# An early store of sixteen zeroed rows ahead of a pooling kernel's main loop

## The chip, the cores and the metric

The kernel runs on one core of a Trainium2 chip. The metric is the device time of one execution in microseconds; the figure used is the median of several runs. Profiles are taken of one execution, and their times count from the first instruction of that execution.

Names used below: ACT is the scalar engine, DVE the vector engine, POOL is GpSimd, SP the engine that here only issues transfers. SBUF is the on-chip memory with 128 partitions, PSUM the smaller one beside it, DRAM the chip's main memory. A transfer (DMA) is issued from an engine's queue (here SP's, which the profile calls q1, or ACT's, q10) and carried out by 16 DMA engines.

## The reference

The reference is a one-dimensional pooling with the 2-norm over windows of four neighbours. With `x` of shape 32 x 256 x 4096 in float32 (134.2 MB), `p = 2` and `kernel_size = 4`:

```python
for i in range(out_length):
    start = i * kernel_size
    end = start + kernel_size
    window = np.abs(x[:, :, start:end]) ** p
    result[:, :, i] = (np.mean(window, axis=-1)) ** (1.0 / p)
```

So every output element is the square root of the mean of four squares. The output is 32 x 256 x 1024 in float32, 33.6 MB.

## The kernel before

Input and output are treated as flat. The input is cut into 20 tiles of 128 partitions. Most are W = 13184 columns wide (52,736 bytes to a partition, 6592 KB in all); tile 3 is 32 columns narrower, and tile 19 takes what is left (11680 columns). R = W / 4 = 3296 is the number of output columns of a full tile.

Tiles are grouped in blocks (`blocks`, L51): four blocks of four tiles, one of three (18, 16, 17) and the last tile alone. A block is one contiguous region of the flat input and of the flat output. Within it each partition owns one contiguous run, so one store writes the results of a whole block, 128 rows of up to 52,736 bytes. `rows(flat, b, div)` (L64) gives the view of block `b` in the input (`div` 1) or the output (`div` 4).

In SBUF there are three input tiles `xt` (L58), used in turn: tile `i` uses slot `i % 3`. The result tile `ot` (L59) has room for four tiles' results; tile `i` of the first 16 writes columns `i % 4 * R` onward (L70), so tiles 0, 4, 8 and 12 share columns 0 to 3295. The sums of tiles 4, 8, 12 and 16 go to a PSUM tile `st` instead, since the columns in `ot` are still being stored then, and their roots are written to `ot` later. Results of the last four tiles are held in a freed input slot.

Each tile passes through four steps:

- a load issued by SP (`load`, L79 to L83);
- the square in place on ACT (`square`, L89);
- two additions on DVE: `pairs` (L95) halves the row, `fours` (L99) writes the sum of four to the result's place;
- the square root with the factor 1/4 on ACT (`root`, L102), for one or several tiles at once.

The first three loads are issued ahead of the loop. After the sums of tile `i`, SP issues load `i + 3` into the slot that was just freed. The stores of blocks 0, 1 and 2 (`store`, L85 and L86) are issued from ACT's queue after the last root of the block, those of blocks 3, 4 and 5 from SP's.

The order is written out by hand: each engine executes its instructions in the order of the program text. Waits are inserted where one instruction touches what another engine or a transfer has written or reads. `implied` (L118) takes out a few of them that other waits cover. Transfers signal their end on eight semaphores that are used in turn. Ahead of the loop ACT computes the root of a constant into `first` (L129), and the load of its function table stands in front of that.

Of the kernel before, what the change touches and what calls it, by code (L numbers as in the profile page):

```python
# [1 line left out]

# [4 lines left out]


@with_exitstack
def kernel(  # L10
    ctx: ExitStack,
    tc: tile.TileContext,
    x: bass.AP,
    p: float,
    kernel_size: int,
    out: bass.AP,
):

    nc = tc.nc

    assert float(p) == 2.0, "kernel specialized for p == 2"
    k = int(kernel_size)  # L30
    assert k == 4, "kernel specialized for kernel_size == 4"

    P = nc.NUM_PARTITIONS
    fp32 = mybir.dt.float32
    Act = mybir.ActivationFunctionType
    add = mybir.AluOpType.add
    xf = x.rearrange("b c l -> (b c l)")
    of = out.rearrange("b c l -> (b c l)")
    total = xf.shape[0] // P

    W = 13184
    R = W // k
    X_SLOTS = 3
    NARROW = W - 32
    LAST = total - 18 * W - NARROW
    widths = [W] * 3 + [NARROW] + [W] * 15 + [LAST]
    n = len(widths)
    assert 0 < LAST <= W and LAST % 16 == 0


    blocks = [[0, 1, 2, 3], [4, 5, 6, 7], [8, 9, 10, 11], [12, 13, 14, 15], [18, 16, 17], [19]]  # L51
    block_of = {i: b for b, group in enumerate(blocks) for i in group}
    block_width = [sum(widths[i] for i in group) for group in blocks]

    x_pool = ctx.enter_context(tc.tile_pool(name="x_pool", bufs=1))
    o_pool = ctx.enter_context(tc.tile_pool(name="o_pool", bufs=1))
    s_pool = ctx.enter_context(tc.tile_pool(name="s_pool", bufs=1, space=bass.MemoryType.PSUM))
    x_tiles = [x_pool.tile([P, W], fp32, name=f"xt{j}") for j in range(X_SLOTS)]  # L58
    o_tile = o_pool.tile([P, 4 * R], fp32, name="ot")  # L59
    first = o_pool.tile([P, 1], fp32, name="first")  # L60
    s_tile = s_pool.tile([P, 4096], fp32, name="st")
    ctx.enter_context(tc.manual_schedule())

    def rows(flat, b, div):  # L64
        at = sum(block_width[:b]) * P // div
        return flat[at:at + block_width[b] * P // div].rearrange("(p w) -> p w", p=P)


    free = x_tiles[17 % X_SLOTS]
    place = {i: o_tile[:, i % 4 * R:i % 4 * R + widths[i] // k] for i in range(16)}  # L70
    place[18] = free[:, R:2 * R]
    place[19] = free[:, 0:LAST // k]
    place[16] = free[:, 2 * R:3 * R]
    place[17] = free[:, 3 * R:4 * R]
    held = [o_tile[:, 0:w // k] for w in block_width[:4]] + [free[:, R:4 * R], place[19]]

    xs, loads, stores, sums, squares = {}, {}, {}, {}, {}

    def load(i):  # L79
        b = block_of[i]  # L80
        at = sum(widths[j] for j in blocks[b][:blocks[b].index(i)])
        xs[i] = x_tiles[i % X_SLOTS][:, 0:widths[i]]
        loads[i] = nc.sync.dma_start(out=xs[i], in_=rows(xf, b, 1)[:, at:at + widths[i]])  # L83

    def store(b, queue):  # L85
        stores[b] = queue.dma_start(out=rows(of, b, k), in_=held[b])  # L86

    def square(v):
        return nc.scalar.activation(out=v, in_=v, func=Act.Square)  # L89

    def pairs(v):

        q = v.rearrange("p (n j) -> p n j", j=k)
        h = v[:, 0:v.shape[1] // 2].rearrange("p (n j) -> p n j", j=2)
        return nc.vector.tensor_tensor(out=h, in0=q[:, :, 0:2], in1=q[:, :, 2:4], op=add)  # L95

    def fours(o, v):
        h = v[:, 0:v.shape[1] // 2].rearrange("p (n j) -> p n j", j=2)
        return nc.vector.tensor_tensor(out=o, in0=h[:, :, 0], in1=h[:, :, 1], op=add)  # L99

    def root(o, s):
        return nc.scalar.activation(out=o, in_=s, func=Act.Sqrt, scale=1.0 / k)  # L102

    summed = {i: s_tile[:, 0:R] if i in (4, 8, 12, 16) else place[i] for i in range(n)}

    def roots(*group):
        if len(group) == 1:
            root(place[group[0]], summed[group[0]])
        else:
            v = o_tile[:, group[0] % 4 * R:(group[-1] % 4 + 1) * R]  # L110
            r = root(v, v)
            if group[0] in (5, 9):

                implied(r, stores[block_of[group[0]] - 1])
        if group[-1] in (3, 7, 11):
            store(block_of[group[-1]], nc.scalar)

    def implied(later, earlier):  # L118

        tc.declare_no_dep(later.ins, earlier.ins, reason="implied by the other waits")  # L120

    for i in range(X_SLOTS):
        load(i)


    ahead = {4: (3,), 8: (7,), 12: (11,)}
    behind = {3: [(0, 1, 2)], 7: [(5, 6), (4,)], 11: [(9, 10), (8,)], 14: [(12,)], 15: [(13, 14)], 16: [(15,)]}

    root(first[:, :], nc.const_aps.tensor(1.0, (P, 1), fp32))  # L129
    for i in range(17):  # L130
        if i in ahead:
            roots(*ahead[i])
        s = square(xs[i])
        squares[i] = s
        if i == 3:
            implied(s, squares[0])
        if i in (3, 7, 11):

            for earlier in sums[i - X_SLOTS]:
                implied(s, earlier)  # L140
        for group in behind.get(i, []):
            roots(*group)
        sums[i] = pairs(xs[i]), fours(summed[i], xs[i])
        if i + X_SLOTS < n:
            load(i + X_SLOTS)

    store(3, nc.sync)
    square(xs[17])
    pairs(xs[17])
    fours(summed[17], xs[17])  # L150
    later = {18: 4608, 19: 2000}

    def shared_square(i):
        v = xs[i][:, 0:later[i]]
        nc.vector.tensor_tensor(out=v, in0=v, in1=v, op=mybir.AluOpType.mult)  # L155
        square(xs[i][:, later[i]:widths[i]])

    def shared_pairs(i):
        implied(pairs(xs[i]), loads[i])

    shared_square(18)
    roots(16)
    roots(17)
    shared_pairs(18)
    fours(summed[18], xs[18])
    shared_square(19)
    roots(18)
    store(4, nc.sync)
    shared_pairs(19)
    fours(summed[19], xs[19])  # L170
    roots(19)
    store(5, nc.sync)


# [1 line left out]
_INS = ['x', 'p', 'kernel_size']  # L176
_OUTS = [((32, 256, 1024), 'float32')]

_NUMBERS = {'p': 2.0, 'kernel_size': 4}


# [26 lines left out]
```

## Time and profile before

| what | value |
|---|---|
| median of three runs | 393.97 us (393.89 to 394.08) |
| the profiled execution's span | 392.3 us |
| ACT busy | 274.4 us |
| DVE busy | 218.2 us |
| POOL busy | 0.2 us (four constants) |
| bytes read from and written to DRAM | 134.22 MB and 33.55 MB |
| issue to landing of the three stores from ACT's queue | 36.3 us for the first, median 35.1 us for the other two |

The span is the time between the first and the last instruction that the profiler recorded; it is 1.7 us below the median of the runs. A span on ACT or DVE is the time in which the engine executed. For transfers the profile shows their issue, their landing and, for each queue, the packets that the 16 DMA engines moved. One row of one transfer is one packet; packets under 512 bytes are the signals at a transfer's end, up to 16 for each. In the lists, `[16.56 <-DMA xt<-in_x_dram]` behind an instruction says how long its engine had been idle before it and what ended that.

### The profile page before, as it was taken

What the parts mean: (1) busy time and instruction counts of PE and PEld (TensorE: products, weight loads), DVE (VectorE), ACT (ScalarE), POOL (GpSimd) and SP (SyncE); (2) the same over time, 40 slices, a digit from 0 to 9 for tenths busy, and PEclk for the clock granted to TensorE, in tenths of its full rate; (3) what the DMA queues carried; (4) which work ended last, traced back from release to release, by engine and by line L of the source; (5) the groups of instructions that cost most, each with busy time, mean ns of one, the idle gap of its engine ahead of it and who ended that gap; (6) DMA issues with size and microseconds to landing.
All of it is one profiled execution on the core that took longest, in us unless ns stands there. A gap on an engine that the chain in (4) does not pass through costs nothing.

```text
span 392.3 us, 176 instructions
## 1 busy us (share of the span) xinstructions
DVE 218.2 (56%) x42; ACT 274.4 (70%) x37; POOL 0.2 (0%) x4
## 2 busy tenths in 40 slices
DVE  0009477580693274905942748069418485699970
ACT  1095695979950859799509597995098999969910
POOL 0000000000000000000000000000000000000000
DMA  8999999999999999999999999999999999999997
GB/s 344 430 430 430 430 440 435 452 457 366 430 430 430 430 430 430 430 441 446 452 446 441 436 430 436 430 430 430 430 430 430 430 430 430 430 453 415 430 413 342
DMA packets 3744, 167.77 MB, mean 428 GB/s; under 512 B 416, under 2 KB 416, under 8 KB 416
## 3 DMA queue, kind: packets, MB, share of 16 engines
q1 hardware_dynamic: 3312, 147.53, 87.4%
q10 hardware_dynamic: 432, 20.25, 11.9%
HBM read 134.22 MB, written 33.55 MB: 428 GB/s over the span
## 4 chain that ended last, share of the span: by engine, by line
DMA 43%; ACT 30%; DVE 23%; issue 0%; ACTq 0%; SPq 0%; DVEq 0%
DMA xt<-in_x_dram 43%; ACT xt L89 28%; DVE xt L95 14%; DVE ot L99 5%; DVE xt L99 3%; DVE xt L155 2%; ACT ot L102 2%; ACT xt L102 1%; ACTq L86 0%; SPq L83 0%; DVEq L95 0%
## 5 line engine op out<-in xcount | busy, mean ns | idle before, releaser
L89 ACT ACTIVATE xt<-xt 128x13184 f32<-128x13184 f32 (+3 forms) x20 | 216.7, 10847 | 92.3 <-DMA xt<-in_x_dram 91.0
L95 DVE TENSOR_TENSOR xt<-xt 128x6592 f32<-128x6592 f32 (+2 forms) x20 | 139.7, 6985 | 144.1 <-ACT xt L89 143.9
L99 DVE TENSOR_TENSOR ot<-xt 128x3296 f32<-128x3296 f32 (+1 forms) x13 | 46.7, 3592 | 17.9 <-DMA out_dram<-ot 17.6
L102 ACT ACTIVATE ot<-ot 128x6592 f32<-128x6592 f32 (+3 forms) x8 | 37.2, 4655 | 7.0 <-DVE ot L99 7.0
L102 ACT ACTIVATE xt<-xt 128x3296 f32<-128x3296 f32 (+1 forms) x3 | 8.5, 2836 | 8.8 <-DVE xt L99 8.8
L99 DVE TENSOR_TENSOR st<-xt 128x3296 f32<-128x3296 f32 x4 | 14.4, 3600 | 0.1
L99 DVE TENSOR_TENSOR xt<-xt 128x3296 f32<-128x3296 f32 (+1 forms) x3 | 10.4, 3461 | 0.1
L102 ACT ACTIVATE ot<-st 128x3296 f32<-128x3296 f32 x3 | 8.7, 2898 | 0.0
L155 DVE TENSOR_TENSOR xt<-xt 128x4608 f32<-128x4608 f32 (+1 forms) x2 | 7.2, 3593 | 0.0
L102 ACT ACTIVATE xt<-st 128x3296 f32<-128x3296 f32 x1 | 2.9, 2898 | 0.0
L102 ACT ACT_TABLE_LOAD x1 | 1.3, 1283 | 0.7 <-PEq L189 0.7
L102 ACT ACTIVATE first<-const-float32-1.0 128x1 f32<-128x1 f32 x1 | 0.2, 202 | 0.0
L189 POOL MEMSET const-bfloat16-1.0<- 128x1 bf16 x1 | 0.1, 101 | 0.0
L189 POOL MEMSET const-uint8-127<- 128x1 uint8 x1 | 0.1, 101 | 0.0
L189 POOL MEMSET const-float32-0.0<- 128x1 f32 x1 | 0.1, 98 | 0.2 <-issue 0.2
L189 POOL MEMSET const-float32-1.0<- 128x1 f32 x1 | 0.1, 98 | 0.0
## 6 DMA issues: line engine op xcount, KB each, us to landing
xt<-in_x_dram SPq DMA_DIRECT2D x18, 6592.0 KB, 29.8
out_dram<-ot ACTq DMA_DIRECT2D x2, 6592.0 KB, 35.1
out_dram<-ot SPq DMA_DIRECT2D x1, 6592.0 KB, 37.1
out_dram<-ot ACTq DMA_DIRECT2D x1, 6588.0 KB, 36.3
xt<-in_x_dram SPq DMA_DIRECT2D x1, 6576.0 KB, 24.7
xt<-in_x_dram SPq DMA_DIRECT2D x1, 5840.0 KB, 21.9
out_dram<-xt SPq DMA_DIRECT2D x1, 4944.0 KB, 16.1
out_dram<-xt SPq DMA_DIRECT2D x1, 1460.0 KB, 8.2
```

The costliest lines, as they stand in the source:

```text
L89: return nc.scalar.activation(out=v, in_=v, func=Act.Square)
L95: return nc.vector.tensor_tensor(out=h, in0=q[:, :, 0:2], in1=q[:, :, 2:4], op=add)
L99: return nc.vector.tensor_tensor(out=o, in0=h[:, :, 0], in1=h[:, :, 1], op=add)
L102: return nc.scalar.activation(out=o, in_=s, func=Act.Sqrt, scale=1.0 / k)
L155: nc.vector.tensor_tensor(out=v, in0=v, in1=v, op=mybir.AluOpType.mult)
L189: nc = _bacc.Bacc("TRN2", target_bir_lowering=False, num_devices=1)
```

## The change

Between the first three loads and the loop two instructions are added. GpSimd writes zeros to columns 0 to 3295 of the result tile in all 128 partitions. Then ACT issues a transfer from every eighth partition of these columns (partitions 0, 8, ..., 120) to the corresponding rows of block 0 of the output: 16 rows of 13,184 bytes, 210,944 bytes in all. The store of block 0 later writes the same place in the output with the results. In program order the new transfer precedes `first` on ACT.

```diff
     for i in range(X_SLOTS):
         load(i)
+    BULK = 3296
+    nc.gpsimd.memset(o_tile[:, 0:BULK], 0.0)
+    nc.scalar.dma_start(out=rows(of, 0, k)[0:P:8, 0:BULK], in_=o_tile[0:P:8, 0:BULK])
 
 
     ahead = {4: (3,), 8: (7,), 12: (11,)}
```

The new instructions bring these waits: the transfer waits for the memset; DVE's sum of tile 0 into the same columns waits for the memset and for the transfer; the root over tiles 0 to 2 waits for the transfer. The transfers after load 0 each use the next of the eight semaphores, compared with before. Everything else is unchanged.

## The prediction

> **What bounds the kernel now.** I read the page first, its slices and its queues.
>
> ```profile
> span 392.3 us, 176 instructions
> ...
> DVE 218.2 (56%) x42; ACT 274.4 (70%) x37; POOL 0.2 (0%) x4
> ...
> DMA  8999999999999999999999999999999999999997
> GB/s 344 430 430 430 430 440 435 452 457 366 430 430 430 430 430 430 430 441 446 452 446 441 436 430 436 430 430 430 430 430 430 430 430 430 430 453 415 430 413 342
> ...
> q1 hardware_dynamic: 3312, 147.53, 87.4%
> q10 hardware_dynamic: 432, 20.25, 11.9%
> ```
>
> No compute engine is above 70%, and the DMA digit is 9 in all slices but the first and the last. The two queues' packets take 87.4 + 11.9 = 99.3% of the time of 16 engines. So the DMA engines bound the kernel from end to end, although the chain of waits names ACT and DVE for half of its length. The timeline confirms it by when the squares (L89) start, which is when loads land:
>
> ```profile
> 0.73 1.28 ACT L102 ACT_TABLE_LOAD   x1 [0.73 <-PEq L189]
> 0.73 338.28 SPq L83 DMA_DIRECT2D xt<-in_x_dram  x20
> 2.02 0.20 ACT L102 ACTIVATE first<-const-float32-1.0 128x1 f32<-128x1 f32 x1
> 18.79 11.19 ACT L89 ACTIVATE xt<-xt 128x13184 f32<-128x13184 f32 x1 [16.56 <-DMA xt<-in_x_dram]
> ...
> 34.35 11.19 ACT L89 ACTIVATE xt<-xt 128x13184 f32<-128x13184 f32 x1 [4.38 <-DMA xt<-in_x_dram]
> 37.07 3.59 DVE L99 TENSOR_TENSOR ot<-xt 128x3296 f32<-128x3296 f32 x1
> ...
> 90.31 0.38 ACTq L86 DMA_DIRECT2D out_dram<-ot  x1
> ...
> 144.41 11.19 ACT L89 ACTIVATE xt<-xt 128x13184 f32<-128x13184 f32 x1 [4.36 <-DMA xt<-in_x_dram]
> ...
> 222.22 11.19 ACT L89 ACTIVATE xt<-xt 128x13184 f32<-128x13184 f32 x1 [4.38 <-DMA xt<-in_x_dram]
> ...
> 371.76 11.74 SPq L86 DMA_DIRECT2D out_dram<-xt  x2
> ```
>
> Loads 0 and 1 land 15.56 us apart. From load 7 (144.41) to load 11 (222.22) four loads and one full store go through in 77.81 us, 15.56 each: a store's byte costs what a load's does, and nothing is idle between. One full transfer is 128 rows of 52,736 bytes, 8 per engine if they are shared evenly, so 15.56 / 8 = **1.945 us per row and engine**. The end is saturated too: the last two stores are issued at 371.76 and about 383.2, and by the page's medians to landing (16.1 and 8.2 us) they land at 387.9 and 391.4. The 3.5 us between is the 1460 KB of the last at the full rate (15.56 x 1460 / 6592 = 3.45). Whatever keeps the slowest DMA engine busy longer therefore comes out at the end, undiminished.
>
> One stretch is not regular. From load 3 (65.47) to load 7 is 78.94 us for the same five transfers, 1.13 more than the next cycle. The third view, DMA in 12 us around the first store (issued at 90.31) and then around the second (169.29), shows where:
>
> ```profile
> DMA packets 103, 5.01 MB, mean 417 GB/s; under 512 B 8, under 2 KB 8, under 8 KB 8
> ...
> q1 hardware_dynamic: 71, 3.32, 72.2%
> q10 hardware_dynamic: 32, 1.69, 32.4%
> ...
> DMA packets 115, 5.27 MB, mean 439 GB/s; under 512 B 15, under 2 KB 15, under 8 KB 15
> ...
> q1 hardware_dynamic: 76, 3.22, 61.9%
> q10 hardware_dynamic: 39, 2.06, 39.5%
> ```
>
> In the first window 95 rows take 104.6% of 12 us x 16 engines, which is 2.11 us a row; in the second 100 rows take 101.4%, which is 1.95. The excess is 95 x 0.16 / 16 = about **1.0 us per engine**. It comes once, where ACT's queue (q10) is used for the first time; the second store has none.
>
> **The change, part by part.**
>
> *The memset.* GpSimd is free after its four constants at 0.43 us. No row shows 3296 columns on it. The bounds are its own 0.10 us for one column and, doubling the nearest row (DVE's 3.59 us for 3296 columns), 7.2 us. I take 3.6, so it ends near 4.3. Nothing else is on GpSimd, and DVE first works at 30.01.
>
> *ACT's queue.* The DMA waits for the memset and stands ahead of the table load (1.28) and `first` (0.20). With 0.38 us for the issue, ACT is through at 4.3 + 0.38 + 1.48 = 6.2 us, or 9.8 with the long memset. Its next work is the square at 18.79, so the waiting costs nothing. Were that cover gone, square 0 would be late and load 3 (issued at 40.70 once DVE has summed tile 0) with it; but load 2 feeds the engines until 49.94, another 9.2 us of cover.
>
> *New waits.* DVE's sum into columns 0 to 3295 (37.07) now waits for the memset and for the early store, and so does the root over tiles 0 to 2. Behind the sum stand load 3 on SP and all later sums. The first full store landed 36.3 us after its issue with 8 rows per engine, each taking turns with a load's. A quarter-length row issued near 4.7 should be in by 15, 22 us before it is needed. The later transfers move on by one among the eight DMA semaphores; load 6 waits for one that load 0 had finished. I cost these at nothing.
>
> *The bytes.* 16 rows of 13,184 bytes are 210,944 bytes that go to DRAM twice. A quarter row takes 1.945 / 4 = 0.486 us on one engine. The trace doesn't show which engine, or which path into the result tile, serves partitions 0, 8, 16 and so on. The ends are 0.49 us (one row to each, nothing shared) and, with two rows in each shared lane, 0.97 us. I take **0.97**, for a reason in the trace: the engines run nearly in step (in the windows their packet starts come in bursts every 1.95 us), so these rows move at the same time, and a load lands only when its last engine is through. If any pair shares a lane, the worst pair counts and not the mean.
>
> The Trainium skill has a rule for each end. "DMA: Bandwidth & Descriptors", section "Why a DMA increments its semaphore by 16 and not by 1", lets a transfer use the largest number of engines up to 16 that divides both sides' outermost size; for 16 rows that is 16 engines, and by it alone the term is 0.49. "SBUF — State Buffer", section "Door 1: The DMA port swizzle", makes bandwidth follow the ports that the partitions reach; partitions eight apart reach 8 of 16, and by it the term is 0.97. No row of this trace shows a transfer of fewer than 128 partitions, so neither is borne out here yet.
>
> *First use of q10.* The 1.0 us moves from 92 us to about 5 us. Engines are as saturated there (422 GB/s in each 2 us from 4 on), so it is paid there and given back at the first full store. Ends: -1.0 (it hides in the first load's own start) and +1.0 (paid at both). I take 0.
>
> **Sum.** Span 392.3 + 0.97 = 393.2. The median of the runs is 393.97, 1.7 above this span; the same distance gives **394.94**, which is 0.25% slower. The bound for telling it from no change is 0.2%, 0.79 us, so 394.76.
>
> **Rivals.**
>
> (a) One row to each engine and no shared lane: 393.97 + 0.49 = **394.46**, not slower by the bound. For it: every transfer here keeps 16 engines equally busy. Against: all of those have 128 rows. A partial overlap of pairs lies between, near 394.7.
>
> (b) The first-use cost comes twice, since q10 then stands idle from about 15 to 90 us: 394.46 + 1.0 to 394.94 + 1.0, **395.4 to 395.9**. Against: about 43 us of idleness (from the first store's landing at 126.6 to 169.3) brought no second one; 75 us is not shown.
>
> (c) The first-use cost hides in the start: the first load needs 18.06 us instead of 15.56, so 2.5 us there aren't transfer. **393.5 to 393.9**. Against: by 4 us the rate is full, and the memset most likely ends later; only a memset well under 3 us would bring the store in earlier.
>
> (d) Few engines take all the rows: four of them with 4 rows each give 1.94 us, 395.9; one with 16 gives 16 x 0.486 = 7.8, **401.8**. Nothing in the trace speaks for it.
>
> (e) The early store waits behind the three queued loads and lands at 50. DVE's sum would be 13 us late, load 3 issued near 53.6 instead of 40.7, and the engines idle for some 4 to 5 us: **about 399**. Against: the first full store landed at 126.6, before load 6, which had been issued ahead of it and landed at 128.86.
>
> **How the numbers follow.** Forecast 0.40; (a) with the partial overlaps 0.31; (b) 0.14; (c) 0.09; (d) and (e) together 0.04; something that I don't see and that is faster, 0.02. The forecast lies only 0.18 us above the bound, so I count 0.03 of it as no change. Slower: 0.37 + 0.14 + 0.04 = 0.55. No change: 0.31 + 0.03 + 0.08 = 0.42. Faster: 0.03, since even (c) at its best is -0.5 us, 0.12%. The range takes in (a), the forecast and (b): 394.2 to 395.9; it leaves out (c), (d), (e) and a little of (b).
>
> **What would show it.** In the changed kernel's profile: load 0 landing near 19.7 instead of 18.79 (19.3 by (a)), plus up to 1.0 if first use is paid there; the cycle from load 3 to load 7 back at 77.8 instead of 78.94; the later cycles unchanged; DVE's first sum not waiting for a DMA; and the memset over well before 10 us. The early store's landing less than 11 us after its issue would clear (e). I am wrong if the cycle from load 3 to load 7 keeps its 1.1 us, or if load 0 is late by no more than the first use and half a microsecond.

## The result and the profile after

The changed kernel takes 394.97 us (median of 9 runs, 394.66 to 395.57) against 393.97 us before (393.87 to 394.18). The ratio is 1.0026, interval 1.0018 to 1.0034: slower by 1.0 us. The profiled execution has a span of 393.0 us; it took 395.06 us.

The page of the changed kernel, slices and queues:

```profile
span 393.0 us, 181 instructions
...
DMA  9999999999999999999999999999999999999997
...
q1 hardware_dynamic: 3312, 147.53, 87.2%
q10 hardware_dynamic: 464, 20.46, 12.0%
```

The engines that move data are as full as before: 99.2% over a span that is 0.7 us longer. q10 has 32 packets more, 16 rows and 16 signals, so 16 engines took part in the early store. The timeline of the changed kernel:

```profile
0.73 2.84 POOL L125 MEMSET ot<- 128x3296 f32 x1 [0.29 <-POOLq L192]
...
3.61 0.58 ACTq L126 DMA_DIRECT2D out_dram<-ot  x1
4.22 1.28 ACT L102 ACT_TABLE_LOAD   x1 [4.22 <-POOL ot L125]
...
19.41 11.19 ACT L89 ACTIVATE xt<-xt 128x13184 f32<-128x13184 f32 x1 [13.69 <-DMA xt<-in_x_dram]
...
37.76 3.59 DVE L99 TENSOR_TENSOR ot<-xt 128x3296 f32<-128x3296 f32 x1
...
66.11 11.16 ACT L89 ACTIVATE xt<-xt 128x13152 f32<-128x13152 f32 x1 [4.34 <-DMA xt<-in_x_dram]
...
144.97 11.19 ACT L89 ACTIVATE xt<-xt 128x13184 f32<-128x13184 f32 x1 [4.41 <-DMA xt<-in_x_dram]
...
222.82 11.19 ACT L89 ACTIVATE xt<-xt 128x13184 f32<-128x13184 f32 x1 [4.40 <-DMA xt<-in_x_dram]
```

The memset and the issue are over long before ACT has anything else to do, and DVE's first sum stands without an idle time in front of it, so the new waits cost no time in the loop. Load 0 lands at 19.41 instead of 18.79, 0.62 later; load 3 is late by 0.64, load 7 by 0.56, load 11 by 0.60. The loss inside the span is made in the first 19 us and carried to the end. The cycle from load 3 to load 7 takes 78.86 us, hardly less than the 78.94 before.

The DMA view of the first 12 us of the changed kernel, queue by queue (packets, MB, share of 16 engines):

```profile
q1 hardware_dynamic: 80, 4.22, 88.1%
q10 hardware_dynamic: 32, 0.21, 4.2%
...
out_dram<-ot ACTq DMA_DIRECT2D x1, 206.0 KB, 8.0
```

The same view of the kernel before:

```profile
q1 hardware_dynamic: 80, 4.22, 87.2%
```

4.2% of 12 us is 0.50 us per engine, signal included: each row takes what a quarter of a 1.945 us row takes, 0.49 us, and no more. In the trace's list of packets each of them follows another load row without a gap, one on each of the 16 engines. The load rows' 88.1% against 87.2% says little. The kernel with the memset and no transfer (below) shows as much in its first 12 us:

```profile
q1 hardware_dynamic: 80, 4.22, 88.0%
```

The first row of an engine takes some 2 to 3 us, and how long varies from run to run. A small price does show in the list of packets: the load row just ahead of an early row took up to 2.30 us instead of 1.95. This is 0.14 us per engine on average here and 0.07 in a second profile of the same kernel; with the memset alone these rows take 1.95 us on every engine. So load 0's delay of 0.62 us is the 0.49 of the early row and about 0.1 of stretched load rows and scatter. The scatter is not small: in the six kernels that move no extra bytes, load 0 landed between 18.79 and 18.95 us five times, and once at 19.30. Nothing here took twice its time.

Inside the span this leaves 0.6 to 0.7 us of the 1.0. The rest is outside: over all runs of this study the time lay about 1.8 us above the span for the kernel before (1.74 to 1.84), and 2.02 to 2.09 us above it in the nine runs of the changed one. One run of all that follow, of the kernel with 16 neighbours, was in a slower state (401.21 us) and is left out of the table.

### The profile page after: what moved, and what is told of

Its sections match the earlier page's. It is cut to its first block, busy times and chain, and to the rows that moved or that the text cites. A ratio compares the mean times of both kernels' runs of the same rounds, so it can differ in the third digit from the quotient of the medians.

```text
span 393.0 us, 181 instructions
## 1 busy us (share of the span) xinstructions
DVE 218.2 (56%) x42; ACT 274.4 (70%) x37; POOL 3.0 (1%) x5
## 3 DMA queue, kind: packets, MB, share of 16 engines
q1 hardware_dynamic: 3312, 147.53, 87.2%
## 4 chain that ended last, share of the span: by engine, by line
DMA 43%; ACT 30%; DVE 23%; issue 0%; ACTq 0%; DVEq 0%; SPq 0%
DMA xt<-in_x_dram 43%; ACT xt L89 28%; DVE xt L95 14%; DVE ot L99 5%; DVE xt L99 3%; DVE xt L158 2%; ACT ot L102 2%; ACT xt L102 1%; ACTq L86 0%; SPq L83 0%; DVEq L95 0%; DVEq L99 0%
## 5 line engine op out<-in xcount | busy, mean ns | idle before, releaser
L89 ACT ACTIVATE xt<-xt 128x13184 f32<-128x13184 f32 (+3 forms) x20 | 216.7, 10847 | 89.3 <-DMA xt<-in_x_dram 88.1
L125 POOL MEMSET ot<- 128x3296 f32 x1 | 2.8, 2844 | 0.3 <-POOLq L192 0.3
```

The source lines that it names most:

```text
L125: nc.gpsimd.memset(o_tile[:, 0:BULK], 0.0)
```

## The experiments

Each was timed in five rounds beside the kernel before on the same chip. "Distance" is the median of time less span over the runs; the last column is the number of instructions that the trace records on DVE, with those that only wait.

| kernel | time | before | ratio, interval | span (before) | distance (before) | DVE |
|---|---|---|---|---|---|---|
| changed kernel again | 395.06 | 394.05 | 1.0024, 1.0015 to 1.0034 | 393.0 (392.3) | 2.05 (1.77) | 54 |
| memset alone | 394.35 | 394.05 | 1.0007, 0.9998 to 1.0016 | 392.3 (392.3) | 2.05 (1.77) | 54 |
| short rows | 394.46 | 394.05 | 1.0010, 1.0001 to 1.0019 | 392.4 (392.3) | 2.07 (1.77) | 54 |
| 16 neighbours | 394.91 | 394.05 | 1.0024, 1.0013 to 1.0034 | 392.8 (392.3) | 2.07 (1.77) | 54 |
| one column on GpSimd | 394.22 | 393.93 | 1.0007, 0.9998 to 1.0016 | 392.2 (392.1) | 2.05 (1.81) | 54 |
| memset on DVE | 394.96 | 393.93 | 1.0024, 1.0015 to 1.0032 | 392.8 (392.1) | 2.17 (1.81) | 55 |
| two rows | 394.58 | 393.93 | 1.0013, 1.0005 to 1.0022 | 392.5 (392.1) | 2.04 (1.81) | 54 |
| narrow tile at 7 | 394.03 | 393.93 | 1.0003, 0.9994 to 1.0012 | 392.2 (392.1) | 1.81 (1.81) | 53 |
| `first` twice | 394.11 | 394.04 | 1.0000, 0.9991 to 1.0009 | 392.3 (392.25) | 1.79 (1.79) | 53 |
| many rows | 394.91 | 394.04 | 1.0022, 1.0013 to 1.0031 | 392.9 (392.25) | 2.03 (1.79) | 54 |
| constant rows | 394.15 | 394.04 | 1.0001, 0.9992 to 1.0010 | 392.4 (392.25) | 1.77 (1.79) | 53 |
| store on SP, spare column | 394.73 | 394.04 | 1.0020, 1.0011 to 1.0029 | 392.7 (392.3) | 2.07 (1.80) | 54 |

### Taking the change apart: no transfer, the whole, short rows

The changed kernel was run again as it is:

> The changed kernel once more, beside runs of the kernel before whose spans are listed. Expected +1.0 us in time again. If the whole loss is DMA work inside the span, the spans differ by as much as the times; the trace so far shows only 0.6 to 0.7 us inside (load 0 lands 0.62 later), so the rest, 0.3 to 0.4, may lie outside or be the scatter of single executions.

It lost 1.0 us again, 0.7 in the span and 0.28 outside it. Next, without the transfer:

```diff
-    nc.scalar.dma_start(out=rows(of, 0, k)[0:P:8, 0:BULK], in_=o_tile[0:P:8, 0:BULK])
```

> The memset stays, the early transfer is gone. If all of the loss comes from the transfer, the time is that of the kernel before, within 0.2 us, and load 0 lands at 18.8. If GpSimd's memset itself or the wait on ACT costs something outside the profiled span, the time is 0.3 to 0.5 us above the kernel before with the span unchanged.

The span is that of before, and the time is 0.30 us higher. The interval of the ratio just takes in 1, but the distances don't overlap: 2.02 to 2.10 us in the eleven runs, 1.74 to 1.83 in the 28 of the kernel before. The memset takes 2.85 us in which nothing waits for it; the price is outside the profiled span. Then the transfer with short rows:

```diff
-    nc.scalar.dma_start(out=rows(of, 0, k)[0:P:8, 0:BULK], in_=o_tile[0:P:8, 0:BULK])
+    nc.scalar.dma_start(out=rows(of, 0, k)[0:P:8, 0:128], in_=o_tile[0:P:8, 0:128])
```

> The same 16 partitions with 512 bytes in each instead of 13,184, so the bytes' own time is 0.02 us per engine. If the loss is the bytes, 0.49 us of it goes and what stays is the change-over between queues, 0.1 to 0.2 us. If a transfer has a fixed price on the engines or outside the span, most of the 1.0 us stays.

This adds 0.11 us to the memset alone, which is about the scatter: the medians of the kernel before differ by 0.12 us between the rounds. Going from 512 to 13,184 bytes in a row adds the rest, 395.06 - 394.46 = 0.60 us, close to the 0.49 us of a row and the 0.07 to 0.14 of stretched load rows read above. So the loss is 0.30 (outside the span) + 0.11 + 0.60 = 1.01 us, each part good to about 0.1.

### Do rows share a lane?

```diff
-    nc.scalar.dma_start(out=rows(of, 0, k)[0:P:8, 0:BULK], in_=o_tile[0:P:8, 0:BULK])
+    nc.scalar.dma_start(out=rows(of, 0, k)[0:16, 0:BULK], in_=o_tile[0:16, 0:BULK])
```

> The same 16 rows of 13,184 bytes, but partitions 0 to 15 in place of every eighth. Theory of shared lanes: sixteen neighbours reach fewer of the lanes than partitions eight apart, four rows to a lane, so the term grows to about 4 x 0.49 = 1.9 us and load 0 lands near 20.8. Theory of one row to an engine with nothing shared: each row again takes 0.49 us, load 0 lands at 19.4, the time is that of the changed kernel.

The time is that of the changed kernel within 0.15 us, and the 1.9 us of the theory are not there. Some sharing shows all the same. In the first 12 us of this kernel:

```profile
q1 hardware_dynamic: 80, 4.22, 87.6%
q10 hardware_dynamic: 32, 0.21, 5.0%
```

q10's rows take 5.0% instead of 4.2%, 0.60 us each on average with the signal. In the trace eight of them take the plain 0.49 us and the others 0.56 to 0.79. For partitions eight apart every row took 0.49. So the rows of neighbours took a little longer and those of partitions eight apart did not. That neighbours share a path is one reading of it, from one profile; a doubling is shown for neither.

### Does the slowest engine set the end?

```diff
-    nc.scalar.dma_start(out=rows(of, 0, k)[0:P:8, 0:BULK], in_=o_tile[0:P:8, 0:BULK])
+    nc.scalar.dma_start(out=rows(of, 0, k)[0:16:8, 0:BULK], in_=o_tile[0:16:8, 0:BULK])
```

> Only partitions 0 and 8 are stored early: 2 rows of 13,184 bytes, an eighth of the bytes. If the slowest DMA engine sets the end, as the prediction has it, two engines that are each 0.49 us late cost as much as sixteen: span near 392.9, time near 394.9. If the bytes count as a sum over 16 engines, the term is 0.06 us and the time is that of the short rows, 394.46.

With an eighth of the bytes, on two engines (two rows and two signals, the four packets of q10 in the first 12 us below), the span still grows by 0.4 us of the 0.6 to 0.7.

```profile
q10 hardware_dynamic: 4, 0.03, 0.5%
```

The time, 394.58, lies between the two that were on record, 394.9 for the slowest engine and 394.46 for the sum, so it doesn't decide between them. The growth of the span is several times the 0.06 of a sum over 16 engines, and less than 0.49. The trace tells more. Load 0 is hardly late:

```profile
19.02 11.19 ACT L89 ACTIVATE xt<-xt 128x13184 f32<-128x13184 f32 x1 [12.72 <-DMA xt<-in_x_dram]
```

With the memset alone it landed at 18.91. In the list of packets the engines are up to 0.6 us apart at this point. The two that took the early rows began them at 8.40 and 8.46 us, when the slowest of the others had until 8.81 with its third load row. They were through at 8.89 and 8.95 and from then on the last, but by 0.14 us only. So the slowest engine does set the landing, as the prediction said, but an early row costs its whole 0.49 us only where it falls on the slowest engine, as it must when all 16 have one. In these two profiles the lateness is 0.11 us at load 0, 0.24 at load 11 and 0.3 at the end of the span; what adds to it on the way isn't shown.

### What costs time outside the span?

First one column on GpSimd and no transfer:

```diff
-    BULK = 3296
+    BULK = 1
     nc.gpsimd.memset(o_tile[:, 0:BULK], 0.0)
-    nc.scalar.dma_start(out=rows(of, 0, k)[0:P:8, 0:BULK], in_=o_tile[0:P:8, 0:BULK])
```

> No transfer, and GpSimd's memset writes one column in place of 3296. The memset alone left the span at 392.3 us but moved the time from 1.77 to 2.05 us above the span. Theory 1: what lies outside the span grows by one more GpSimd instruction that DVE waits for, whatever its size; the distance is 2.05 again, time 394.35. Theory 2: it grows with the memset's length (2.85 us of GpSimd work); the distance is back at 1.77, time 394.05.

The distance is 2.05 us, so the length of the memset has no part in it. Then the whole change with its memset on DVE:

```diff
-    nc.gpsimd.memset(o_tile[:, 0:BULK], 0.0)
+    nc.vector.memset(o_tile[:, 0:BULK], 0.0)
```

> The changed kernel with the memset on DVE in place of GpSimd; the transfer is unchanged. If the 0.28 us outside the span belong to GpSimd, the distance from span to time is back at 1.77 us, the span stays near 393.0 and the time is 394.75. If any added instruction costs this, distance 2.05 and time 395.05. DVE is free until 30 us, so the span is not expected to change for the memset's sake.

Both guesses failed: the distance is larger, 2.17. It isn't GpSimd's. Then one more instruction on ACT in the kernel before:

```diff
     root(first[:, :], nc.const_aps.tensor(1.0, (P, 1), fp32))
+    root(first[:, :], nc.const_aps.tensor(1.0, (P, 1), fp32))
```

> The kernel before with the root of a constant into the tile first executed twice: one more small instruction, on ACT, and nothing else. A memset of one column on GpSimd moved the time 0.25 us further from the span. Theory 1: any added instruction does that; distance 2.05 us, time 0.25 above before. Theory 2: it takes an engine that was not in the exchange of waits before (GpSimd), so an instruction on ACT leaves the distance at 1.8 and the time within 0.1 us of before.

No change. What the kernels with a larger distance have in common is DVE: the wait for the memset, or for the transfer, is an instruction of its own in front of DVE's first sum. To part the instruction from the wait, the last run put a memset on DVE that nobody waits for. It also has an edit that belongs to the next section, the first full store on SP's queue:

```diff
-            store(block_of[group[-1]], nc.scalar)
+            store(block_of[group[-1]], nc.sync if group[-1] == 3 else nc.scalar)
...
+    spare = o_pool.tile([P, 1], fp32, name="spare")
+    nc.vector.memset(spare[:, :], 0.0)
```

> The kernel before with two unrelated edits that are read in different places. First, one memset of a single column of a spare tile on DVE, which nothing waits for. So far the distance from span to time was 1.8 us where DVE executes 53 recorded instructions, 2.05 where 54 (a wait was added to its sum of tile 0) and 2.17 where 55. If DVE's instructions set it, the distance is 2.05 here; if it was the wait, it is 1.8. Second, the first full store is issued from SP's queue, behind load 6, in place of ACT's. If the extra 1.1 us there belong to ACT's queue, the cycle from load 3 to load 7 is 77.8 us and the span up to 1 us shorter, some 391.3; if they come with the first long store whatever its queue, the cycle stays near 78.9 and the span at 392.2.

The distance is 2.07. One more instruction on DVE, of 0.06 us and waited for by none, moves the time 0.27 us away from the span. This run also had one instruction more on SP; but the memset on DVE gave 2.17 with SP's count as before, and the constant rows below left the distance alone with two more on ACT. In the traces of all these kernels DVE's count is the only one of the four engines' that goes with the distance. What happens in that time isn't recorded, and why DVE's count matters stays open.

### The extra microsecond at the first full store

The other edit of that run belongs here. Timeline of the run with the store on SP:

```profile
65.65 11.16 ACT L89 ACTIVATE xt<-xt 128x13152 f32<-128x13152 f32 x1 [4.34 <-DMA xt<-in_x_dram]
...
90.47 0.35 SPq L86 DMA_DIRECT2D out_dram<-ot  x1
...
144.40 11.19 ACT L89 ACTIVATE xt<-xt 128x13184 f32<-128x13184 f32 x1 [20.02 <-DMA xt<-in_x_dram]
169.35 0.38 ACTq L86 DMA_DIRECT2D out_dram<-ot  x1
...
222.59 11.19 ACT L89 ACTIVATE xt<-xt 128x13184 f32<-128x13184 f32 x1 [4.39 <-DMA xt<-in_x_dram]
```

The first cycle is 78.75 us although ACT's queue hasn't been used yet, so most of the extra comes with the first full store on whichever queue. In the list of packets it is about one load row on each engine, the one just ahead of the store's first row: 2.6 to 3.1 us instead of 1.95 in the kernel before, 2.4 to 3.2 here. In the 13 profiles with the store on ACT's queue the first cycle is 78.5 to 79.0 us, the next one 77.8 to 77.9. Here the next cycle is 78.19 instead of 77.81: ACT's queue, now first used at 169.35, costs another 0.4. In the 12 us from 164 on, the load rows of this run take

```profile
q1 hardware_dynamic: 80, 4.22, 85.4%
```

and in the kernel before, where the queue was in use already,

```profile
q1 hardware_dynamic: 80, 4.22, 81.1%
```

which is 4.3% of 12 us, 0.5 us per engine. So ACT's queue has a price of its own at its first full store, even after one on SP's, and with the store moved the span is 0.4 us longer. That the 1.13 us of the kernel before is made of these two prices isn't shown: here they add up to 0.9 + 0.4 = 1.3. Nor is it shown why a first full store has a price.

Three others tried to move or remove it. The narrow tile at another place:

```diff
-    widths = [W] * 3 + [NARROW] + [W] * 15 + [LAST]
+    widths = [W] * 7 + [NARROW] + [W] * 11 + [LAST]
```

> The kernel before, with the tile that is 32 columns narrower moved from place 3 to place 7, so that block 1 and not block 0 has rows of 52,704 bytes. Theory: the 1.1 us extra at the first full store come from being the first long transfer of ACT's queue; then the cycle from load 3 to load 7 stays at 78.9 us and that from load 7 to load 11 at 77.8. Rival: they come from the odd row length, which moves with the tile; then the first of these cycles is 77.8 and the second 78.9.

The cycles are 78.85 and 77.78 us, so the row's length isn't the cause. The early bytes cut into 128 rows:

```diff
-    nc.scalar.dma_start(out=rows(of, 0, k)[0:P:8, 0:BULK], in_=o_tile[0:P:8, 0:BULK])
+    nc.scalar.dma_start(out=rows(of, 0, k)[:, 0:412], in_=o_tile[:, 0:412])
```

> The changed kernel with the same bytes cut otherwise: 412 columns of all 128 partitions, eight rows of 1,648 bytes for each engine in place of one of 13,184. The bytes' term stays 0.49 us. After 16 early rows the first full store still pays its 1 us (cycle from load 3 to load 7 78.9 us). If that price belongs to the first transfer of 128 rows on ACT's queue, it is now paid at the start: that cycle shrinks to 77.8 and load 0 lands 1 us later than 19.4; the time stays near 395. If it belongs to the first long rows, the cycle stays at 78.9.

The cycle from load 3 to load 7 stays (66.09 to 145.08, 78.99 us), and the time is that of the changed kernel. And 128 rows of 4 bytes at the very start of the kernel before:

```diff
+    nc.scalar.dma_start(out=rows(of, 0, k)[:, 0:1], in_=nc.const_aps.tensor(1.0, (P, 1), fp32), allow_slow_non_contiguous=True)
     for i in range(X_SLOTS):
         load(i)
```

> The kernel before plus one transfer on ACT's queue at the very start, ahead of the first load: 128 rows of 4 bytes (a constant of each partition) into block 0's first output column, no memset and no new engine. Theory: the 1 us at the first full store belongs to the first transfer of 128 rows on this queue, and at the start, where the engines have no packet before 1.7 us, most of it hides; the cycle from load 3 to load 7 is 77.8 us and the time 0.5 to 1.0 us below before. Rival: the price belongs to the first long store, wherever small ones came before; the cycle stays at 78.9 and the time within 0.2 us of before, or a little above.

Again 78.6 us, and no gain. An early small transfer does not pay this price in advance, whether of 16 or 128 rows. Whether an early transfer with full rows would was not tried. No run here beat the kernel before.

## Why the prediction was right, and where its steps were not

The time came out at 394.97 for a forecast of 394.94, but that it is so close is luck: the bytes were put some 0.4 us too high, and 0.28 us outside the span were put at nothing. By the prediction's own sign of being wrong, its account of q10's first use failed: the cycle from load 3 to load 7 kept 1.04 of its 1.13 us. Load 0, at 19.41, lies nearer to the 19.3 of rival (a) than to the 19.7 of the forecast.

**DMA engines bound the kernel from end to end.** Right. The delay of the first load, 0.62 us, is found again at every later landing (0.56 to 0.64) and at the end. That the slowest engine counts agrees with the run of two rows, where two late engines moved the slowest by 0.14 us at load 0 and the span grew by 0.4; that run also shows that the engines aren't in step but up to 0.6 us apart.

**The bytes at 0.97 us.** This step failed. It took two rows in each shared lane. One row to each engine and nothing shared is what the trace shows, 0.49 us as in rival (a); what comes on top is 0.07 to 0.14 us of stretched load rows. Of the two rules weighed there, the Trainium skill's "DMA: Bandwidth & Descriptors" (section "Why a DMA increments its semaphore by 16 and not by 1") is borne out: 16 rows used 16 engines, two rows two. The rule of the Trainium skill's "SBUF — State Buffer" (section "Door 1: The DMA port swizzle"), as the prediction worked it out, would have doubled the rows eight apart; they took 0.49 us each, and 16 neighbours 0.60 on average with the signal. By rows alone the kernel would have been within 0.2% of before.

**The same distance from span to time.** The sum carried the 1.7 us from one profile over as fixed. It grew by 0.28 us, with one more instruction on DVE. This made up most of the 0.37 us by which the bytes fell short: 0.60 + 0.28 + the 0.11 of the short rows is the 1.0.

**First use of q10 moves from 92 us to 5 us and nets to nothing.** Wrong in its mechanism, right in its net. The net was about nothing, but nothing moved: the first full store pays its microsecond after every early transfer that was tried (cycles of 78.5 to 79.0 us), and the early store pays some 0.1 us itself. In the DMA view of the changed kernel from 88 to 100 us the stretch is still there,

```profile
q1 hardware_dynamic: 67, 3.38, 72.9%
q10 hardware_dynamic: 32, 1.69, 32.4%
```

105.3% for 96 rows, 2.11 us a row as before. Reading it as the queue's first use was too quick: what the view showed was the first use of the queue and the first full store at once. This is in number what rival (b) feared, a price at both places, but the early one is small.

**Memset, ACT's wait, DVE's wait at nothing.** Right inside the span: 2.84 us for an assumed 3.6, ACT through at 5.7 instead of 6.2, the store landed 8.0 us after its issue, long before DVE's sum. Rival (e) is out. DVE's wait cost something in a place that the steps did not look at. Rivals (c) and (d) are out too: load 0 was late by 0.6, and 16 engines shared the rows. The 2.5 us that (c) counted as no transfer are in part one: in the kernel before the engines have their first rows from 1.7 us on, and take 2.0 to 3.0 us for each instead of 1.95.

## What to carry to other kernels

Where transfers fill the whole span, a small extra transfer can cost what its longest share on one DMA engine costs, plus a little where it breaks in on rows under way. It costs less where that engine was ahead of the slowest one, and dividing its bytes by the total rate is right only if it is spread over all engines. A time is not only its span: an edit with no cost in the trace can still show in the measured time, so compare the distance between the two as well as the spans. And when a stall coincides with two first events, don't name one of them until they have been parted.

## What was not expected of the hardware

- One more instruction on DVE, of 0.06 us and off every path, made the time 0.27 us longer outside the span; two more gave 0.36. One or two more on ACT, or an extra transfer from ACT's queue that DVE didn't wait for, gave nothing.
- The first full store stretched about one load row on every engine, by 0.7 to 1.1 us on average in the profiles, on SP's queue as on ACT's; a first full store on ACT's queue after one on SP's cost 0.4 to 0.5 us more. Later full stores stretched none, the first on SP's queue behind three on ACT's among them.
- The landing of a transfer under full load follows its rows on an engine and not its bytes. The same 206 KB landed in 8.0 us as 16 rows and in 19.7 us as 128, since each row waits its turn behind a load's row:

```profile
out_dram<-ot ACTq DMA_DIRECT2D x1, 206.0 KB, 19.7
```
